# Another way of loading the first pair of contraction tiles, and row-block roots taken where they are used, in a 2048 x 2048 x 2048 matmul with RMS norm

## The chip, the cores and the metric

The kernel runs on one core of a Trainium2 chip. The metric is the device time of one execution in microseconds (us). The kernel before takes 224.4 us, the median of three runs from 224.26 to 224.63. The profiled execution is one of that kind. Engines are named as the profile names them: PE (TensorE matmul), PEld (its weight load), DVE (VectorE), ACT (ScalarE), POOL (GpSimd), SP (SyncE, which here only issues transfers).

## The reference

```python
m, k, n = 2048, 2048, 2048
x = np.matmul(a, b)
rms = np.sqrt(np.mean(x ** 2, axis=-1, keepdims=True) + eps)
return (gamma * x / rms).astype(np.float32)
```

All inputs and the output are float32 in DRAM. Each row of the product is divided by its own root mean square and multiplied by gamma.

## The kernel before

The 2048 rows are 16 row blocks of 128 rows; the contraction is 16 tiles of 128, taken in eight pairs `kp`. B has a left half (`j=0`) and a right half (`j=1`) of 1024 columns each, or four chunks of 512.

**The head (blocks 0 to 3, plain matmuls).** For each pair `kp`, `load_head` (L105) issues on POOL's software queue a load of A (four blocks by 256 columns, cast to bf16) and a load of B (256 rows by 1024 columns, cast to bf16). POOL issues in program order, and the trace shows that a ninth load waits until the first of the eight before it has landed. The pair 0 is loaded otherwise: A as float32 by SP's hardware queue (L92), B as float32 in two transfers by ACT's hardware queue (L94). `transpose_first` (L143) transposes the float32 A on PE into two PSUM banks, and DVE and ACT cast B (L151, L153) and DVE moves the transposed A to SBUF (L154). Eleven matmuls on zeros (L138) run ahead of it. Then `stream` (L364) runs for every `kp` seven output chunks for each of the two tiles, 14 matmuls; for the next pair's A, eight transposes (`transpose_head`, L160) stand between. The eighth chunk has no accumulating bank: `stream_in_parts` (L378) multiplies its two tiles into the bank `tbank`, which the transposes use too (there is one such bank), and ACT or DVE adds it to x in SBUF. When the left half is done, the same happens for the right half; in it DVE also forms sums of quarters of B (`b_sums`, `b_sums_in_place`, `b_sum_7`), and blocks 4 and 5 are normalised, cast (`prepare`) and transposed on PE by `transpose_half` (L174), again through the one `tbank`.

**The groups (blocks 4 to 15, two blocks each, seven products instead of eight).** `group_half(g, j)` (L483) forms a 2 x 2 block product from seven products of eight matmuls each, in the order 2, 5, 1, 4, 3, 7, 6. Their left operands are sums of quarters of A (`a_sums`, L238, on DVE), their right ones sums of quarters of B. Product 4 accumulates into the bank of product 2, and so must wait until ACT has copied product 2 out (the copy `c`, L498); product 3 likewise waits for DVE's L502, which reads the bank of product 5. Between the products stand hooks 0 to 7, at which `hooks_of` (L535) puts other work: `row_norm` (ACT, squares of a block's rows, then a root), `row_factor` (DVE, four small instructions that wait for it), `apply` (ACT scales and casts a block, L231, then SP issues a transfer that transposes it, L186) and `finish(mb)` (the end of a block: DVE multiplies both halves by 1/rms and gamma, L340, and SP stores them). A group's loads are issued when the group before has written a certain chunk (`load_after`, L529). The last group has its own order (`last_group`).

**The roots.** The sum of a block's squares and its root are `take_rms` (L313): a reduction on DVE, then a square root on ACT. `finish` then needs only a reciprocal on DVE. In groups 3 to 6, `take_rms` of the blocks that will be finished in this group stands at hook 1 of the left half, before the next `row_norm`; elsewhere `finish` calls it itself. The engines take their instructions strictly in the order in which the program issues them, so this order decides who waits for whom.

Of the kernel before, what the change touches and what calls it, by code (L numbers as in the profile page):

```python
# [8 lines left out]
FP32 = mybir.dt.float32  # L9
# [8 lines left out]
def kernel(  # L18
# [13 lines left out]
    nc = tc.nc  # L32
    P = 128
# [30 lines left out]
    sums = [t_left, t_right]  # L64

    a0f = early[:, 0:2048].bitcast(FP32).rearrange("p (r k) -> p r k", r=HB)
    b0f = [early[:, 2048 + t * 2048:2048 + (t + 1) * 2048].bitcast(FP32) for t in range(2)]
    NAH = 6
    ah_slot = [early[:, 6144 + s * 1024:6144 + (s + 1) * 1024].rearrange("p (r k) -> p r k", r=HB)
               for s in range(NAH)]  # L70
# [20 lines left out]

    nc.sync.dma_start(out=a0f, in_=a[0:HB * P, 0:W2].rearrange("(r p) k -> p r k", p=P))  # L92
    for t in range(2):
        nc.scalar.dma_start(out=b0f[t], in_=b[t * P:(t + 1) * P, 0:HALF])  # L94

    def ah(kp):
        return ah_slot[(kp - 1) % NAH]
# [7 lines left out]
    def load_head(kp):  # L105
        nc.gpsimd.dma_start(  # L106
            out=ah(kp),
            in_=a[0:HB * P, kp * W2:(kp + 1) * W2].rearrange("(r p) k -> p r k", p=P))
        load_b(0, kp)
# [10 lines left out]

        nc.gpsimd.tensor_copy(out=pace, in_=src)

    load_head(1)
    identity_f = consts.tile([P, P], FP32, name="identity_f")
    make_identity(nc, identity_f)
    for kp in range(2, 4):
        load_head(kp)
    warm = sq_pool.tile([P, 2 * CH], BF16, name="sq")
    nc.vector.memset(warm, 0.0)
# [4 lines left out]


    warm_bank = ps_a.tile([P, CH], FP32, name="acc")
    for _ in range(11):
        nc.tensor.matmul(warm_bank, warm[:, 0:P], warm[:, 0:CH], start=True, stop=True)  # L138

    gamma_sb = consts.tile([P, N], FP32, name="gamma_sb")  # L140
# [2 lines left out]
    def transpose_first():  # L143
        bank = [ps_t.tile([P, CH], FP32, name="tbank"), ps_a.tile([P, CH], FP32, name="acc")]
        view = [b.rearrange("p (r m) -> p r m", r=HB) for b in bank]
        for t in range(2):
            for r in range(HB):
                nc.tensor.matmul(view[t][:, r, :], a0f[:, r, t * P:(t + 1) * P], identity_f,
                                 is_transpose=True, start=(r == 0), stop=(r == HB - 1))
        for t in range(2):  # L150
            cast_first = [lambda: nc.vector.tensor_copy(out=raw[0][0][:, t, :CH],  # L151
                                                        in_=b0f[t][:, :CH]),
                          lambda: nc.scalar.copy(out=raw[0][0][:, t, CH:], in_=b0f[t][:, CH:])]  # L153
            move = [lambda h=h: nc.vector.tensor_copy(  # L154
                out=head_at[:, t, 2 * h:2 * h + 2, :], in_=view[t][:, 2 * h:2 * h + 2, :])
                for h in range(2)]
            for work in (cast_first + move if t == 0 else move + cast_first):
                work()

    def transpose_head(kp):  # L160
        bank = ps_t.tile([P, CH], FP32, name="tbank")
# [146 lines left out]
    def x_chunk(mb, c):  # L308
        return x_tile(mb, c // 2)[:, (c % 2) * CH:(c % 2 + 1) * CH]

    rms_of = {}

    def take_rms(mb):  # L313

        tot = stat_pool.tile([P, 1], FP32, name="tot")
        nc.vector.reduce_sum(out=tot, in_=msq.pop(mb), axis=mybir.AxisListType.X)
        rms_of[mb] = stat_pool.tile([P, 1], FP32, name="rms")
        nc.scalar.activation(out=rms_of[mb], in_=tot, func=ACTF.Sqrt)

    def inverse(rms):  # L320
        r = stat_pool.tile([P, 1], FP32, name="r")
        nc.vector.reciprocal(out=r, in_=rms)  # L322
        return r

    def inverse_rms(last, partial):

        rms = stat_pool.tile([P, 1], FP32, name="rms")
        nc.scalar.activation(out=rms, in_=last, func=ACTF.Sqrt, bias=partial, scale=1.0)
        return inverse(rms)

    def rows(mb, lo, hi):
        return out[mb * P:(mb + 1) * P, lo:hi]

    def finish(mb, order=(0, 1)):
        if mb not in rms_of:
            take_rms(mb)
        r = inverse(rms_of.pop(mb))
        for h in order:
            x = x_half.pop((mb, h))
            nc.vector.scalar_tensor_tensor(  # L340
                out=x, in0=x, scalar=r, in1=gamma_sb[:, h * HALF:(h + 1) * HALF],
                op0=ALU.mult, op1=ALU.mult)
            nc.sync.dma_start(out=rows(mb, h * HALF, (h + 1) * HALF), in_=x)
# [17 lines left out]
            kind, which = later.pop(0)  # L361
            load_b(1, which) if kind == "b" else load_block(which)

    def stream(groups, kp, before=(), when=None):  # L364


        order = [(g, kt) for kt in (2 * kp, 2 * kp + 1) for g in groups]
        if kp == KP - 1 or (kp == 0 and not before):
            order.sort(key=lambda x: groups.index(x[0]))
        for n, (g, kt) in enumerate(order):  # L370
            if n == (when or len(groups)):
                for work in before:
                    work()
            if kt == 0:
                banks[g] = new_bank()
            head_matmul(banks[g], *g, kt)
# [24 lines left out]
    for kp in range(KP):  # L401
        if kp + 4 < KP:
            load_head(kp + 4)
        else:
            load_later(1)
        before = [lambda: transpose_head(kp + 1)] if kp + 1 < KP else []
        stream(groups1, kp, before, len(groups1) + 5 if kp == 0 else None)
        if kp == KP - 1:
            evict(groups1, (1, 3, 5))
        stream_in_parts(last1, kp)  # L410
        if kp > 0:
            b_sums(0, kp - 1)
    load_later(2)
    b_sums(0, KP - 1)
# [16 lines left out]
    for kp in range(KP):  # L431
        load_later(1)
        before = [lambda: transpose_half(HB, 0)] if kp == 6 else []
        if kp == 7:
            before = [lambda: transpose_half(HB, 1)]
        stream(groups2, kp, before)
        square(squares[kp][0], x_chunk(*squares[kp]))
        if kp == 4:
            prepare(HB)
        if kp == 6:  # L440

            prepare(HB + 1)
        elif kp == KP - 1:
            b_sums_in_place(0, kp - 1)
        else:
            b_sums_2(kp)
    nc.gpsimd.dma_start(out=gamma_sb, in_=gamma.partition_broadcast(P))
    load_block(HB + 2)
    load_block(HB + 3)
# [10 lines left out]
    for kt in range(KT):  # L460
        if kt in (0, 6):
            transpose_half(HB + 1, kt // 6)
            if kt == 0:
                b_sums(1, KP - 2)
                b_sum_7(1, KP - 2)
        head_matmul(bank, r3, 3, kt)
    evict(groups2[-1:], ())
    row_norm(HB + 2)
# [66 lines left out]
    def hooks_of(g, j):  # L535


        hooks = {n: [] for n in range(8)}
        nxt = 2 * g + 2

        def hook(n, work, *args):
            hooks[n].append(lambda: work(*args))

        def apply(mb):
            row_apply(mb)
            transpose_dma(mb)

        more = g + 1 < NG
        if j == 0:
            if g == G0:  # L550
                hook(0, row_factor, nxt)
                hook(1, row_norm, nxt + 1)
                hook(1, apply, nxt)
                hook(2, a_sums, g, (7, 6))
                hook(2, row_factor, nxt + 1)
                hook(2, finish, 1)
                hook(3, squares2, 2)
                hook(4, apply, nxt + 1)
# [178 lines left out]
```

## Time and profile before

| | |
|---|---|
| median of three runs | 224.4 us |
| the profiled execution: time / span of its instructions | 224.4 / 222.6 us |
| PE busy | 211.1 us (95%) |
| DVE busy | 161.8 us (73%) |
| ACT busy | 129.1 us (58%) |
| POOL busy | 24.5 us (11%) |
| moved by transfers | 47.13 MB, mean 212 GB/s |

The span begins with the first instruction and ends with the last; 1.8 us of the execution lie outside it. Times in the trace count from the span's start. A line of the timeline gives start, duration, engine, source line, operation, what it writes and reads, how many instructions, and in brackets how long the engine sat idle before it and what ended that.

### The profile page before, as it was taken

What the parts mean: (1) busy time and instruction counts of PE and PEld (TensorE: products, weight loads), DVE (VectorE), ACT (ScalarE), POOL (GpSimd) and SP (SyncE); (2) the same over time, 40 slices, a digit from 0 to 9 for tenths busy, and PEclk for the clock granted to TensorE, in tenths of its full rate; (3) what the DMA queues carried; (4) which work ended last, traced back from release to release, by engine and by line L of the source; (5) the groups of instructions that cost most, each with busy time, mean ns of one, the idle gap of its engine ahead of it and who ended that gap; (6) DMA issues with size and microseconds to landing.
All of it is one profiled execution on the core that took longest, in us unless ns stands there. A gap on an engine that the chain in (4) does not pass through costs nothing.

```text
span 222.6 us, 3026 instructions
## 1 busy us (share of the span) xinstructions
PE 211.1 (95%) x1043; PEld 98.6 (44%) x1043; DVE 161.8 (73%) x324; ACT 129.1 (58%) x272; POOL 24.5 (11%) x49
## 2 busy tenths in 40 slices
PE   7899999999999999999999999999999999999950
PEld 2445444444454444444444444444444444444430
DVE  2427557983999989978949298837994589587692
ACT  3110002807698895799646985699478954334570
POOL 7534232300000001000100002000200000000000
PEclk9999999999999999999999999999999999999997
DMA  6999999999973499818889259945994794044045
GB/s 184 223 202 209 203 208 211 212 303 259 327 280 159 188 272 292 310 72 226 276 228 400 58 174 222 366 151 143 246 368 168 97 282 189 0 188 193 0 190 188
DMA packets 36176, 47.13 MB, mean 212 GB/s; under 512 B 21952, under 2 KB 26048, under 8 KB 34496
## 3 DMA queue, kind: packets, MB, share of 16 engines
q0 software_dynamic: 9648, 23.33, 41.6%
q1 hardware_dynamic: 26080, 22.29, 33.0%
q10 hardware_dynamic: 432, 1.31, 2.0%
q8 instruction: 8, 0.13, 0.2%
q14 instruction: 8, 0.07, 0.1%
HBM read 34.60 MB, written 16.78 MB: 231 GB/s over the span
## 4 chain that ended last, share of the span: by engine, by line
PE 83%; DMA 8%; DVE 2%; POOL 2%; issue 1%; ACT 1%; DVEq 0%; ACTq 0%; POOLq 0%
PE acc L279 63%; PE acc L350 18%; DMA b<-in_b_dram 8%; POOL early L106 1%; DVE x L617 1%; POOL b L100 1%; DVE x L620 1%; PE tbank L179 1%; PE tbank L382 1%; PE tbank L165 1%; ACT sq L291 0%; DVEq L732 0%; ACT sq L682 0%; DVE x L690 0%; DVE r L322 0%
## 5 line engine op out<-in xcount | busy, mean ns | idle before, releaser
L279 PE MATMUL acc<-b,s 128*128 128x512 bf16 x376 | 83.3, 379 | 0.0
L279 PEld LDWEIGHTS <-s 128*128 128x128 f16 x472 | 46.2, 98 | 55.7 <-DVE s L244 0.2
L350 PE MATMUL acc<-b,head_at 128*128 128x512 bf16 x240 | 55.1, 379 | 0.6 <-DMA b<-in_b_dram 0.4
L291 ACT ACTIVATE sq<-x 128x512 bf16<-128x512 f32 x62 | 39.1, 631 | 10.9 <-DVE x L520 5.1
L340 DVE SCALAR_TENSOR_TENSOR x<-x,r,gamma_sb 128x1024 f32<-128x1024 f32 x28 | 34.7, 1282 | 0.8
L209 ACT ACTIVATE sq<-a 128x1024 bf16<-128x1024 f32 x24 | 25.4, 1057 | 16.8 <-DMA a<-in_a_dram 16.4
L350 PEld LDWEIGHTS <-head_at 128*128 128x128 bf16 x240 | 22.9, 98 | 26.7 <-issue 1.1
L393 ACT COPY x<-acc 128x512 f32<-128x512 f32 x11 | 5.9, 591 | 25.1 <-PE acc L350 25.1
L231 ACT ACTIVATE head_at<-a,s 128x2048 f16<-128x2048 f32 x10 | 19.9, 1990 | 0.0
L279 PEld LDWEIGHTS <-at_even 128*128 128x128 f16 x96 | 9.4, 98 | 11.5 <-issue 0.4
L279 PEld LDWEIGHTS <-head_at 128*128 128x128 f16 x96 | 9.4, 98 | 11.3
L100 POOL DMA_DIRECT2D b<-in_b_dram x15 | 10.6, 708 | 16.0 <-DMA b<-in_b_dram 13.2
L217 DVE TENSOR_SCALAR s<-norm 128x1 f32<-128x1 f32 x12 | 1.8, 150 | 14.3 <-ACT norm L212 14.2
L244 DVE TENSOR_TENSOR s<-at_even 128x1024 f16<-128x1024 f16 x15 | 9.7, 684 | 2.8 <-DMA at_even<-head_at 2.8
L291 ACT ACTIVATION_READ_ACCUMULATOR sq<-x 128x1 f32 x62 | 11.7, 188 | 0.0
L279 PE MATMUL acc<-t_left,s 128*128 128x512 bf16 x48 | 11.3, 379 | 0.0
L279 PE MATMUL acc<-early,s 128*128 128x512 bf16 x48 | 11.3, 379 | 0.0
L279 PE MATMUL acc<-early,at_even 128*128 128x512 bf16 x48 | 11.0, 379 | 0.0
L279 PE MATMUL acc<-t_left,at_even 128*128 128x512 bf16 x48 | 10.9, 379 | 0.0
L509 ACT COPY x<-acc 128x512 f32<-128x512 f32 x10 | 5.7, 575 | 8.9 <-PE acc L279 8.9
L279 PE MATMUL acc<-t_left,head_at 128*128 128x512 bf16 x48 | 10.8, 379 | 0.0
L279 PE MATMUL acc<-early,head_at 128*128 128x512 bf16 x48 | 10.8, 379 | 0.0
(86 smaller groups left out, 205.8 us busy)
## 6 DMA issues: line engine op xcount, KB each, us to landing
out_dram<-x SPq DMA_DIRECT2D x30, 512.0 KB, 3.1
a<-in_a_dram POOLq DMA_DIRECT2D x12, 1024.0 KB, 8.5
b<-in_b_dram POOLq DMA_DIRECT2D x15, 512.0 KB, 17.1
early<-in_a_dram POOLq DMA_DIRECT2D x7, 256.0 KB, 14.8
early<-in_b_dram ACTq DMA_DIRECT2D x2, 512.0 KB, 5.9
gamma_sb<-in_gamma_dram POOLq DMA_DIRECT2D x1, 1024.0 KB, 19.9
out_dram<-x SPq DMA_DIRECT2D x3, 256.0 KB, 3.5
early<-in_a_dram SPq DMA_DIRECT2D x1, 512.0 KB, 5.7
```

The costliest lines, as they stand in the source:

```text
L100: nc.gpsimd.dma_start(out=raw[j][kp], in_=b[kp * W2:(kp + 1) * W2, j * HALF:(j + 1) * HALF].rearrange("(t p) n -> p t n", p=P))
L106: nc.gpsimd.dma_start(out=ah(kp), in_=a[0:HB * P, kp * W2:(kp + 1) * W2].rearrange("(r p) k -> p r k", p=P))
L165: nc.tensor.matmul(view[:, t, r, :], ah(kp)[:, r, t * P:(t + 1) * P], identity, is_transpose=True, start=(t == 0 and r == 0), stop=(t == 1 ...
L209: nc.scalar.activation(out=junk, in_=a32[mb][:, h * HALF:(h + 1) * HALF], func=ACTF.Square, scale=2.0 ** -8, accum_out=n2[:, h:h + 1])
L231: nc.scalar.activation(out=a16[mb], in_=a32.pop(mb), func=ACTF.Copy, scale=factor.pop(mb))
L244: nc.vector.tensor_tensor(out=s_sum[s], in0=x, in1=y, op=op)
L279: nc.tensor.matmul(bank, lhsT[:, kp, :], rhs, start=(start and kp == 0), stop=(kp == KP - 1), skip_group_check=not start)
L291: nc.scalar.activation(out=sq[:, 0:CH], in_=src, func=ACTF.Square, scale=inv_sqrt_n, accum_out=msq[mb][:, c:c + 1])
L340: nc.vector.scalar_tensor_tensor(out=x, in0=x, scalar=r, in1=gamma_sb[:, h * HALF:(h + 1) * HALF], op0=ALU.mult, op1=ALU.mult)
L350: nc.tensor.matmul(bank, head_at[:, kt, r, :], head_rhs(c, kt), start=(kt == 0), stop=(kt == KT - 1))
L393: copy(out=x_chunk(*g), in_=banks[g])
L509: nc.scalar.copy(out=x21, in_=p2)
```

## The change

In the head, B of pair 0 is no longer loaded as float32 and cast by DVE and ACT: POOL's software queue casts it in two transfers, and these are POOL's first. The load of A and B of pair 1 moves behind the making of the identity matrix. The warm-up has 8 matmuls. The transposed A of the first tile is moved by DVE, that of the second by ACT. In pair 0, the eighth chunk is multiplied after the seven matmuls of the first tile, and the transposes of pair 1 come three matmuls later, where they stood five later and the eighth chunk last.

At the end of the right half, `b_sums(1, 6)` and `b_sum_7(1, 6)` come before the last evictions instead of behind the first transposes of block 5.

In groups 3 to 6, the reduction and the root of a block are taken inside `finish`, never ahead of it; `row_factor` of the group's second new block moves from hook 2 to hook 3, and in group 3 `finish(3)` stands first at hook 2.

```diff
-    b0f = [early[:, 2048 + t * 2048:2048 + (t + 1) * 2048].bitcast(FP32) for t in range(2)]
...
     for t in range(2):
-        nc.scalar.dma_start(out=b0f[t], in_=b[t * P:(t + 1) * P, 0:HALF])
+        nc.gpsimd.dma_start(out=raw[0][0][:, t, :], in_=b[t * P:(t + 1) * P, 0:HALF])
...
-    load_head(1)
     identity_f = consts.tile([P, P], FP32, name="identity_f")
     make_identity(nc, identity_f)
-    for kp in range(2, 4):
+    for kp in range(1, 4):
         load_head(kp)
...
-    for _ in range(11):
+    for _ in range(8):
...
         for t in range(2):
-            cast_first = [lambda: nc.vector.tensor_copy(out=raw[0][0][:, t, :CH],
-                                                        in_=b0f[t][:, :CH]),
-                          lambda: nc.scalar.copy(out=raw[0][0][:, t, CH:], in_=b0f[t][:, CH:])]
...
+            move = (nc.vector.tensor_copy, nc.scalar.copy)[t]
+            for h in range(2):
+                pair = slice(2 * h, 2 * h + 2)
+                move(out=head_at[:, t, pair, :], in_=view[t][:, pair, :])
...
-    def take_rms(mb):
...
+    def inverse_rms(last, partial=None):
+
+        rms = stat_pool.tile([P, 1], FP32, name="rms")
+        if partial is None:
+            tot = stat_pool.tile([P, 1], FP32, name="tot")
+            nc.vector.reduce_sum(out=tot, in_=msq.pop(last), axis=mybir.AxisListType.X)
+            nc.scalar.activation(out=rms, in_=tot, func=ACTF.Sqrt)
+        else:
+            nc.scalar.activation(out=rms, in_=last, func=ACTF.Sqrt, bias=partial, scale=1.0)
         r = stat_pool.tile([P, 1], FP32, name="r")
         nc.vector.reciprocal(out=r, in_=rms)
         return r
...
     def finish(mb, order=(0, 1)):
-        if mb not in rms_of:
-            take_rms(mb)
-        r = inverse(rms_of.pop(mb))
+        r = inverse_rms(mb)
...
-            if n == (when or len(groups)):
+            if n == len(groups) + late:
                 for work in before:
                     work()
+            if late and n == len(groups):
+                stream_in_parts(last1, kp)
...
-        stream(groups1, kp, before, len(groups1) + 5 if kp == 0 else None)
+        stream(groups1, kp, before, 3 if kp == 0 else 0)
         if kp == KP - 1:
             evict(groups1, (1, 3, 5))
-        stream_in_parts(last1, kp)
         if kp > 0:
+            stream_in_parts(last1, kp)
             b_sums(0, kp - 1)
...
-        elif kp == KP - 1:
-            b_sums_in_place(0, kp - 1)
         else:
-            b_sums_2(kp)
+            b_sums_2(min(kp, KP - 2))
...
             transpose_half(HB + 1, kt // 6)
-            if kt == 0:
-                b_sums(1, KP - 2)
-                b_sum_7(1, KP - 2)
...
-                done = [2 * g - 2, 2 * g - 1]
+                if g == G0 + 1:
+                    hook(2, finish, r3)
                 hook(0, row_factor, nxt)
                 hook(1, apply, nxt)
-                if g == G0 + 1:
-                    hook(2, finish, r3)
-                    done.insert(0, r3)
-                for mb in done:
-                    hook(1, take_rms, mb)
                 hook(1, row_norm, nxt + 1)
-                hook(2, row_factor, nxt + 1)
+                hook(3, row_factor, nxt + 1)
                 hook(4 if g == G0 + 1 else 3, finish, 2 * g - 2)
```

More of the change, by code (lines that the diff above doesn't have):

```diff
@@ L150, in transpose_first @@
         for t in range(2):
-            cast_first = [lambda: nc.vector.tensor_copy(out=raw[0][0][:, t, :CH],
-                                                        in_=b0f[t][:, :CH]),
-                          lambda: nc.scalar.copy(out=raw[0][0][:, t, CH:], in_=b0f[t][:, CH:])]
[L154 to L158, printed above, removed]
+            move = (nc.vector.tensor_copy, nc.scalar.copy)[t]
+            for h in range(2):
+                pair = slice(2 * h, 2 * h + 2)
+                move(out=head_at[:, t, pair, :], in_=view[t][:, pair, :])
     def transpose_head(kp):
@@ L309, in x_chunk @@
         return x_tile(mb, c // 2)[:, (c % 2) * CH:(c % 2 + 1) * CH]
-    rms_of = {}
-    def take_rms(mb):
[L315 to L320, printed above, removed]
+    def inverse_rms(last, partial=None):
[6 more added lines that the diff above has]
+            nc.scalar.activation(out=rms, in_=last, func=ACTF.Sqrt, bias=partial, scale=1.0)
         r = stat_pool.tile([P, 1], FP32, name="r")
@@ L323, in inverse @@
         return r
[L325 to L329, printed above, removed]
     def rows(mb, lo, hi):
@@ L362, in load_later, with stream @@
             load_b(1, which) if kind == "b" else load_block(which)
-    def stream(groups, kp, before=(), when=None):
+    def stream(groups, kp, before=(), late=0):
         order = [(g, kt) for kt in (2 * kp, 2 * kp + 1) for g in groups]
```

## The prediction

> **What bounds the kernel now.** I read the chain of work that ended last, then the transfers by queue in the head, then the timeline at the three places that the change touches. The chain in order of time:
>
> ```profile
> 7.18 17.47 DMA b<-in_b_dram
> 24.64 0.04 issue
> 24.69 1.67 PE acc L350 x7
> ...
> 69.41 140.08 PE acc L279 x648
> ```
>
> Until 24.64 the chain is loading; from 24.69 to 209.5 it is PE without a gap, at 1.73 us for a product of eight matmuls. So a microsecond counts in two forms: PE starts earlier or later on the loads, or PE gets a wait that it does not have now. The other engines have slack, and it must be read at each place.
>
> The queues in the first 6.6 us (packets, MB, share of 16 engines), and the head's timeline:
>
> ```profile
> q10 hardware_dynamic: 201, 0.76, 40.7%
> q1 hardware_dynamic: 528, 0.52, 23.7%
> q0 software_dynamic: 3, 0.00, 0.2%
> ```
>
> ```profile
> 1.25 0.88 POOL L106 DMA_DIRECT2D early<-in_a_dram  x1 [0.80 <-POOLq L718]
> ...
> 10.00 0.77 POOL L106 DMA_DIRECT2D early<-in_a_dram  x1 [2.08 <-DMA early<-in_a_dram]
> ...
> 12.38 1.67 PE L350 MATMUL acc<-b,head_at 128*128 128x512 bf16 x7
> ...
> 12.63 0.70 POOL L100 DMA_DIRECT2D b<-in_b_dram  x1 [1.86 <-DMA b<-in_b_dram]
> 13.85 0.77 POOL L106 DMA_DIRECT2D early<-in_a_dram  x1 [0.52 <-DMA early<-in_a_dram]
> ...
> 16.32 0.70 POOL L100 DMA_DIRECT2D b<-in_b_dram  x1 [1.71 <-DMA b<-in_b_dram]
> ```
>
> POOL issued its first load at 1.25, yet the software queue moved three packets before 6.6, while the hardware queues had the engines. POOL's waits show when loads land: A of pair 1 by 10.00, B by 12.63, the next by 13.85 and 16.32. So a pair takes 3.85 (10.00 to 13.85), an A about 1.35, a B 2.5. PE needs 3.9 for a pair (18.24 to 22.14) and trails the loads by a few tenths, with one 0.4 wait at 24.69. Loads and PE are in step, and whatever moves the loads moves PE.
>
> The end of the right half, on DVE and PE, then the left half of group 3 on ACT, DVE and PE:
>
> ```profile
> 64.44 0.68 DVE L269 TENSOR_TENSOR b<-b 128x1024 bf16<-128x1024 bf16 x1
> 65.55 0.69 DVE L183 COPY at_even<-tbank 128x1024 f16<-128x1024 f16 x1 [0.43 <-PE tbank L179]
> 66.16 1.09 DVE L254 TENSOR_TENSOR early<-b 128x512 bf16<-128x512 bf16 x3
> ...
> 66.65 0.61 PE L179 MATMUL tbank<-identity_h,x 128*128 128x128 f16 x8
> ```
>
> ```profile
> 100.46 0.16 DVE L322 RECIPROCAL r<-rms 128x1 f32<-128x1 f32 x1 [1.21 <-ACT rms L318]
> 102.87 0.29 ACT L212 ACTIVATE norm<-n 128x1 f32<-128x1 f32 x1
> 104.30 1.99 ACT L231 ACTIVATE head_at<-a,s 128x2048 f16<-128x2048 f32 x1
> 107.64 0.59 ACT L498 COPY x<-acc 128x512 f32<-128x512 f32 x1
> 110.90 3.62 PE L279 MATMUL acc<-early,head_at 128*128 128x512 bf16 x16
> 116.41 1.89 DVE L244 TENSOR_TENSOR s<-at_even 128x1024 f16<-128x1024 f16 x3 [2.79 <-DMA at_even<-head_at]
> ```
>
> The reader is to see small margins: `tbank` is free at 66.24 and PE wants it at 66.65; copy `c` of the right half is done at 108.2 and product 4 starts at 110.90, a slack of 2.7.
>
> **Part 1, the head.** Removed: two float32 loads on ACT's queue, four casts, three warm-up matmuls (0.43 each). These matmuls end at 5.38, with PE idle until 6.57, so their removal is worth nothing by itself. They start 0.43 apart until 4.0 and twice as fast from about 4.4, so eight end near 4.7 and still reach the faster pace. Added: two software loads, which together are one B, 2.5 of the queue, ahead of pair 1. POOL's issues are 0.7 to 0.9 each, and pair 1's are done by about 5, before the queue reaches them. The casts' cover goes nowhere: DVE and ACT idle there.
>
> What matters is T, when the software queue starts. B of pair 1 then lands at T + 2.5 + 3.85; now PE has it by 12.3. Earliest T: 1.25 plus the 1.8 that a later load on an idle queue took (issued 88.37, moving at 90.18) = 3.05; latest: as now, about 6.6. Now it began when SP's A (0.52 MB) had finished, at about 6.35. With A alone on hardware, starting at about 2 and at the 300 GB/s that q1 reached alone, A is through by 4.3, and the queue joins 0.3 to 1.0 later. I take T = 5.1, nearest to that row: B lands at 11.45, **0.85 earlier**. PE can follow: A's transposes from 4.9, first matmul near 6.9, pair 1 from about 11. Ends: 6.6 and a slow start, as the queue now takes until 8.4 to fill, cost up to 0.9; 3.05 gains at most 1.4, since A then shares packets with 4 KB rows of B as now, lands near 6.2, and PE itself reaches pair 1 at 11.4 (1.0), without the 0.4 wait later. The eighth chunk moved up is the same two matmuls, 0.43; its ACT copy (0.59) must free `tbank` before the transposes, which the three matmuls between (0.65) cover.
>
> Here the Trainium skill bears on T. "DMA: Bandwidth & Descriptors", Latency and other measured facts, gives a first byte after about 1 us on the software path and 0.6 on the hardware one. By that T would be 3.1 and the head part a gain of 1.4 instead of 0.85; the trace's first load, 5.4 from issue to data, does not agree.
>
> **Part 2, the end of the right half.** Three L254 (0.40 apart) and one L259 (0.34 until the next) move ahead of the L183 that frees `tbank`. DVE has no pause from 55.18 to 65.1, so L183 starts at 64.44 + 0.60 + 1.20 + 0.34 = 66.58 and ends at 67.27. PE's second transposes wait from 66.65 until 67.33: **0.68 later**. Bounds: 0.2 if DVE leads more, 0.9. The first sums of A then have room, since L183 and L244 follow at once: no second wait.
>
> **Part 3, the roots.** The instructions are the same; only waits change. At group 3, left half, `finish(3)` needs a root that now stands behind the second `row_norm` on ACT. That ends at 103.07, or 102.8 without the three roots ahead of it (0.28). Root 0.2, reciprocal at 103.05 instead of 100.46; the two L340 take 2.40, until 105.65; then L506 (0.60), `row_factor` (0.70), L511 (0.60) and block 4's reduction (0.15): 107.7. ACT has done its copy and square by 104.4 and now stands before block 4's root until 107.7, with `apply` of block 9, the copy of product 3 and the right half's `c` queued behind. So `apply` starts at 107.95 instead of 104.30; 1.89, 0.6 and 0.8 later `c` starts at 111.2 and ends at 111.8. PE wants product 4 at 110.90: **0.9 wait**.
>
> Next late is the transposed block 9. SP issues it behind block 4's stores, whose second L340 ends at 110.65 instead of 107.87; so 111.1 instead of 108.41. It then took 8.0 until L244 began (116.41). The same gives 119.1, the first sum 0.7 later at 119.8; PE starts group 4 at 117.8 (121.26 less two products), now 118.7. The wait is 1.1, or 0.3 with the 7.2 that the same step took in group 4; I take **0.7**. Then L525 is late by 3, so POOL's loads for group 5 are late by 2.5, and `row_norm` holds ACT before `c` in group 4: slack there was 0.9 (c done 122.08, product 4 at 122.98), and the like happens in its right half: **0.25** in both. From group 5 on one `finish` per half delays ACT by 1.0 against slacks of 1.9 and more: nothing. Sum 1.85, bounds 0 (all absorbed by slack I read too small) and 3.
>
> Moving `row_factor` to hook 3 lets L506 go first: its bank is needed only three products later, so nothing.
>
> **Sum** against the profiled execution (224.4, which is also the median): -0.85 + 0.68 + 1.85 = +1.7, so **226.1 us**. Tail and last group issue the same work in the same order: 0.
>
> **Rivals.**
> 1. The software queue needs its 5.4 us after the first issue whatever else runs. For it: that is all the trace shows of a first load. Against: the queue came alive just when A had ended. Head +0.9 instead of -0.85: 227.8. It decides from T = 5.95 on, where the head turns to a loss.
> 2. The queue starts promptly, T near 3. For it: 1.8 at 88.37. Against: 6.6. Head -1.4: 225.5. (By the skill's first byte this is the case to expect.)
> 3. Not slower: ACT's stand before block 4's root does not reach PE. For it: group 2 has two inline roots in its left half now, and `c` there keeps 1.7 of slack; PE has seven banks. Against: group 3 starts with ACT already late (its `c` ends at 97.06, 1.7 after product 2) and finishes one block more. Price: part 3 falls to 0, total -0.17: 224.2. It decides once less than 0.2 of the 1.85 is left. With rival 2 on top it is 223.7.
> 4. The head does not do what it says, as PE is held by pair 4's load as before: that is T = 5.95, head 0: 227.0, inside the range.
>
> **Chances.** Forecast 0.45, rival 1 0.2 (with rival 4), rival 2 0.12, rival 3 0.15, rivals 2 and 3 together 0.08. The measurement tells 0.2%, 0.45 us. Faster: 0.08 from the last and 0.06 from rival 3; same 0.1, 0.07 of it from rival 3 and the rest from the forecast's low end; slower the rest, 0.76. The range reaches from rival 3 to just past rival 1, 223.9 to 228.1; the forecast's own is 225.2 to 227.0.
>
> **What would show it.** Pair 1's matmuls at about 11.5 and software packets from about 5; a 0.7 gap on PE at the second transposes of block 5, released by DVE L183; ACT idle some 3 us before a root in group 3's left half, and PE waiting about 0.9 for ACT L498; PE waiting for L244 at the start of group 4. Wrong would be PE without waits after 70 us, or software packets only from 6.6.

## The result and the profile after

The changed kernel takes 227.84 us (median of four runs, 227.6 to 228.21) against 224.5 (224.26 to 224.63) for the kernel before in the same session: a ratio of 1.0151, 95% interval 1.0134 to 1.0169, or 3.3 us more. Forecast were 226.1, in a range from 223.9 to 228.1. The sign was right and the time lies inside the range, close to its upper end; the loss is twice the +1.7 that the sum gave. The profiled execution is the 227.6 one, with a span of 225.8 us (222.6 before), so it has to explain 3.2 us.

In the kernel after, the head's matmul is L335 (was L350), the groups' product L273 (L279), copy `c` L481 (L498), the sums of A L238 (L244), the move of `tbank` L177 (L183), the root L311 (L318), the reciprocal L315 (L322), `apply` L225 (L231), the transposing transfer L180 (L186), the load of B L99 and of A L105. The chain of work that ended last, its long pieces in order of time (start, duration, what):

```profile
8.86 16.01 DMA b<-in_b_dram
25.16 15.76 DMA b<-in_b_dram
41.20 21.04 DMA b<-in_b_dram
...
112.04 8.03 DMA at_even<-head_at
...
120.85 91.70 PE acc L273 x424
```

Before, PE carried the chain without a gap from 24.69 on. Now the loads of B carry it until 62.2, and a transposing transfer carries it at the start of group 4. PE's list of waits (total, times, longest, in us) says the same by name; first its one wait for a load before, then after:

```profile
PE acc L350 <- DMA b<-in_b_dram: 0.4, 1, 0.4
```

```profile
PE acc L335 <- DMA b<-in_b_dram: 3.5, 4, 1.4
...
PE acc L273 <- DVE s L238: 1.3, 1, 1.3
PE acc L273 <- ACT x L481: 0.5, 1, 0.5
...
PE tbank L173 <- DVE at_even L177: 0.2, 1, 0.2
```

**The head.** First the first 6.6 us of the queues (packets, MB, share of 16 engines), and the issue of B's first pair (KB each, median us from issue to landing):

```profile
q0 software_dynamic: 221, 0.41, 45.9%
q1 hardware_dynamic: 528, 0.52, 25.7%
...
b<-in_b_dram POOLq DMA_DIRECT2D x2, 256.0 KB, 6.2
```

The software queue, three packets before, has moved 221 packets by 6.6; its first two are at 3.3 us. But it moves them slowly. The stretches of the after kernel (busy time of PE, PEld, DVE, ACT, POOL; granted PE clock; share of the DMA engines; GB/s, in bytes as written):

```profile
4.00:6.00 2.00, 1.57 (x11) 1.18 (x10) 0.76 (x2) 0.39 (x2) 2.00 (x4) 1.00 0.98 130
6.00:8.00 2.00, 1.00 (x5) 0.48 (x5) 0.00 (x0) 0.25 (x1) 2.00 (x7) 1.00 1.02 129
8.00:10.00 2.00, 1.81 (x10) 0.65 (x8) 0.00 (x0) 0.59 (x1) 1.00 (x2) 1.00 1.30 207
```

The hardware queue's last packets are at 3.8, so from 4 to 8 us the software queue has the engines to itself and moves 130 GB/s; the same kind of load moves 207 from 8 us on. The timeline shows what PE makes of it:

```profile
1.24 1.21 POOL L93 DMA_DIRECT2D b<-in_b_dram  x2 [0.79 <-POOLq L697]
...
7.00 1.67 PE L335 MATMUL acc<-b,head_at 128*128 128x512 bf16 x7 [1.43 <-DMA b<-in_b_dram]
...
8.86 0.70 POOL L99 DMA_DIRECT2D b<-in_b_dram  x1 [0.56 <-DMA b<-in_b_dram]
...
10.18 0.77 POOL L105 DMA_DIRECT2D early<-in_a_dram  x1 [0.62 <-DMA early<-in_a_dram]
...
12.46 1.67 PE L335 MATMUL acc<-b,head_at 128*128 128x512 bf16 x7 [1.03 <-DMA b<-in_b_dram]
...
24.91 1.67 PE L335 MATMUL acc<-b,head_at 128*128 128x512 bf16 x7 [0.59 <-DMA b<-in_b_dram]
```

B of pair 0 lands by 7.0 and 8.86, A of pair 1 by 10.18, B of pair 1 by 12.46, where PE waits 1.03 for it. Pair 1 so starts where it did (12.38), although PE began its first matmul 0.7 earlier than before (7.00 against 7.71).

**The end of the right half.** PE and DVE:

```profile
62.28 1.67 PE L335 MATMUL acc<-b,head_at 128*128 128x512 bf16 x7 [0.46 <-DMA b<-in_b_dram]
...
65.04 0.68 DVE L263 TENSOR_TENSOR b<-b 128x1024 bf16<-128x1024 bf16 x1
65.64 1.09 DVE L248 TENSOR_TENSOR early<-b 128x512 bf16<-128x512 bf16 x3
...
67.11 0.68 DVE L177 COPY at_even<-tbank 128x1024 f16<-128x1024 f16 x1
67.84 0.61 PE L173 MATMUL tbank<-identity_h,x 128*128 128x128 f16 x8 [0.20 <-DVE at_even L177]
```

PE waits for the last pair of B, which it did not before, and then for `tbank`, which the sums hold up.

**Group 3, left half, and the start of group 4.**

```profile
103.99 0.16 DVE L315 RECIPROCAL r<-rms 128x1 f32<-128x1 f32 x1 [4.49 <-ACT rms L311]
...
108.67 0.20 ACT L311 ACTIVATE rms<-tot 128x1 f32<-128x1 f32 x1 [3.48 <-DVE tot L310]
...
111.90 0.57 ACT L481 COPY x<-acc 128x512 f32<-128x512 f32 x1
112.04 3.41 SPq L180 DMA_TRANSPOSE at_even<-head_at  x1
...
112.52 3.61 PE L273 MATMUL acc<-early,head_at 128*128 128x512 bf16 x16 [0.47 <-ACT x L481]
...
120.10 1.90 DVE L238 TENSOR_TENSOR s<-at_even 128x1024 f16<-128x1024 f16 x3 [2.26 <-DMA at_even<-head_at]
120.85 3.63 PE L273 MATMUL acc<-b,s 128*128 128x512 bf16 x16 [1.26 <-DVE s L238]
```

DVE stands 4.49 before block 3's reciprocal, ACT then stands 3.48 before block 4's root, `c` ends at 112.47, and PE waits 0.47 for it. The transposed block 9 comes at 120.10, and PE waits 1.26 for its sum.

The same places in both timelines, in us, and how far behind the forecast had PE there:

| PE starts | before | after | behind | forecast |
|---|---|---|---|---|
| pair 1 | 12.38 | 12.46 | +0.08 | -0.85 |
| pair 4 | 24.69 | 24.91 | +0.22 | -0.85 |
| last pair of the right half (before: seventh of the 13 matmuls from 60.14, 0.216 apart) | 61.43 | 62.28 | +0.85 | -0.85 |
| second transposes of block 5 | 66.65 | 67.84 | +1.19 | -0.17 |
| product 4 of group 3 | 110.90 | 112.52 | +1.62 | +0.73 |
| product 1 of group 4 | 121.26 | 124.31 | +3.05 | +1.43 |
| end of the span | 222.6 | 225.8 | +3.2 | +1.7 |

After group 4's start hardly anything is lost. At 62 us PE is 1.7 behind the forecast; what follows adds 2.35 (3.2 less 0.85) where the forecast had 2.53 (0.68 + 1.85).

### The profile page after: what moved, and what is told of

It reads as the page before. It is cut to its first block, busy times and chain, and to the rows that moved or that the text cites. A ratio compares the mean times of both kernels' runs of the same rounds, so it can differ in the third digit from the quotient of the medians.

```text
span 225.8 us, 3015 instructions
## 1 busy us (share of the span) xinstructions
PE 210.6 (93%) x1040; PEld 98.3 (44%) x1040; DVE 160.4 (71%) x320; ACT 128.9 (57%) x272; POOL 25.6 (11%) x51
## 4 chain that ended last, share of the span: by engine, by line
PE 41%; DMA 34%; issue 12%; DVE 6%; ACT 4%; POOL 1%; DVEq 0%; POOLq 0%; ACTq 0%
PE acc L273 41%; DMA b<-in_b_dram 26%; DMA a<-in_a_dram 4%; DMA at_even<-head_at 4%; DVE x L325 2%; DVE x L596 1%; ACT sq L203 1%; ACT head_at L225 1%; DVE x L599 1%; ACT sq L285 1%; ACT x L380 0%; POOL a L114 0%; DVE s L238 0%; DVE r L315 0%; DVE x L494 0%
## 5 line engine op out<-in xcount | busy, mean ns | idle before, releaser
L273 PE MATMUL acc<-b,s 128*128 128x512 bf16 x376 | 83.4, 379 | 1.3 <-DVE s L238 1.3
L273 PEld LDWEIGHTS <-s 128*128 128x128 f16 x472 | 46.1, 98 | 57.2 <-DVE s L238 1.8
L335 PE MATMUL acc<-b,head_at 128*128 128x512 bf16 x240 | 55.4, 379 | 3.5 <-DMA b<-in_b_dram 3.5
L335 PEld LDWEIGHTS <-head_at 128*128 128x128 bf16 x240 | 23.0, 98 | 29.6 <-issue 3.9
L380 ACT COPY x<-acc 128x512 f32<-128x512 f32 x11 | 5.9, 591 | 29.2 <-PE acc L335 29.2
L225 ACT ACTIVATE head_at<-a,s 128x2048 f16<-128x2048 f32 x10 | 19.9, 1990 | 0.0
L273 PEld LDWEIGHTS <-head_at 128*128 128x128 f16 x96 | 9.4, 98 | 12.0 <-issue 0.8
L273 PEld LDWEIGHTS <-at_even 128*128 128x128 f16 x96 | 9.4, 98 | 11.3
L99 POOL DMA_DIRECT2D b<-in_b_dram x15 | 10.6, 707 | 16.1 <-DMA b<-in_b_dram 13.8
L164 DVE COPY head_at<-tbank 128x1024 bf16<-128x1024 bf16 x7 | 4.8, 692 | 10.0 <-PE tbank L159 10.0
L273 PE MATMUL acc<-t_left,s 128*128 128x512 bf16 x48 | 11.3, 379 | 0.0
L273 PE MATMUL acc<-early,s 128*128 128x512 bf16 x48 | 11.3, 379 | 0.0
L238 DVE TENSOR_TENSOR s<-at_even 128x1024 f16<-128x1024 f16 x15 | 9.7, 684 | 2.3 <-DMA at_even<-head_at 2.3
L273 PE MATMUL acc<-early,head_at 128*128 128x512 bf16 x48 | 10.8, 379 | 0.5 <-ACT x L481 0.5
L120 POOL COPY pace<-x 128x1 f32<-128x1 f32 x4 | 0.7, 183 | 90.4 <-DVE x L508 90.4
L273 PE MATMUL acc<-early,at_even 128*128 128x512 bf16 x48 | 10.9, 379 | 0.0
L273 PE MATMUL acc<-t_left,head_at 128*128 128x512 bf16 x48 | 10.8, 379 | 0.0
L273 PE MATMUL acc<-t_left,at_even 128*128 128x512 bf16 x48 | 10.8, 379 | 0.0
```

The lines of the kernel that those rows point to most:

```text
L99: nc.gpsimd.dma_start(out=raw[j][kp], in_=b[kp * W2:(kp + 1) * W2, j * HALF:(j + 1) * HALF].rearrange("(t p) n -> p t n", p=P))
L164: nc.vector.tensor_copy(out=head_at[:, 2 * kp:2 * kp + 2, :, :], in_=view)
L225: nc.scalar.activation(out=a16[mb], in_=a32.pop(mb), func=ACTF.Copy, scale=factor.pop(mb))
L238: nc.vector.tensor_tensor(out=s_sum[s], in0=x, in1=y, op=op)
L273: nc.tensor.matmul(bank, lhsT[:, kp, :], rhs, start=(start and kp == 0), stop=(kp == KP - 1), skip_group_check=not start)
L335: nc.tensor.matmul(bank, head_at[:, kt, r, :], head_rhs(c, kt), start=(kt == 0), stop=(kt == KT - 1))
```

## The experiments

Each run is compared with runs of the kernel before on the same chip; chips differ between some of the runs.

### Each part alone

**head_only: part 1 alone on the kernel before.**

```diff
-    b0f = [early[:, 2048 + t * 2048:2048 + (t + 1) * 2048].bitcast(FP32) for t in range(2)]
...
-        nc.scalar.dma_start(out=b0f[t], in_=b[t * P:(t + 1) * P, 0:HALF])
+        nc.gpsimd.dma_start(out=raw[0][0][:, t, :], in_=b[t * P:(t + 1) * P, 0:HALF])
...
-    for _ in range(11):
+    for _ in range(8):
...
-        stream(groups1, kp, before, len(groups1) + 5 if kp == 0 else None)
+        stream(groups1, kp, before, 3 if kp == 0 else 0)
```

> The kernel before with part 1 alone. By the prediction, 0.85 us faster. By the reading of the trace after, the first B rows move at half the steady rate, pair 1 starts where it did, and B of the right half's last pair lands late: 0.2 to 0.9 us slower, with a wait of PE on a load of B near 62 us.

Measured: 225.89 us, ratio 1.0063 (1.0046 to 1.0081), that is +1.45. Its profiled execution (226.54) in the timeline, and one stretch of it with the columns as above:

```profile
9.16 3.09 PE L344 MATMUL acc<-b,head_at 128*128 128x512 bf16 x7 [2.79 <-DMA b<-in_b_dram]
```

```profile
10.00:12.00 2.00, 2.00 (x6) 0.66 (x5) 0.00 (x0) 0.00 (x0) 0.87 (x2) 0.50 1.16 201
```

B of pair 0 is later still than in the kernel after, PE idles 2.79 before its first matmul, and then runs on half the clock (0.50): seven matmuls take 3.09 where they took 1.67. So part 1 is a loss by itself, greater than both expectations, and it begins with B's late landing; how much of it the half clock adds is read under head_warm. The expected wait near 62 us is not in this profile: PE is already 2.0 late there.

**sums_only: part 2 alone.**

```diff
-        elif kp == KP - 1:
-            b_sums_in_place(0, kp - 1)
         else:
-            b_sums_2(kp)
+            b_sums_2(min(kp, KP - 2))
...
-            if kt == 0:
-                b_sums(1, KP - 2)
-                b_sum_7(1, KP - 2)
```

> The kernel before with part 2 alone. By the prediction 0.7 us slower: PE waits at the second transposes of block 5 for the DVE copy that frees tbank, from 66.65 to about 67.33. The rival reads the trace after, where that wait was 0.2 to 0.4: then at most 0.4 us slower.

Measured: 224.9, ratio 1.0019 (1.001 to 1.0028), +0.46, which is nearer to the rival's 0.4 than to the 0.7. PE's waits have the one that was forecast:

```profile
PE tbank L179 <- DVE at_even L183: 0.4, 1, 0.4
```

**roots_only: part 3 alone.**

```diff
-                done = [2 * g - 2, 2 * g - 1]
-                hook(0, row_factor, nxt)
-                hook(1, apply, nxt)
                 if g == G0 + 1:
                     hook(2, finish, r3)
-                    done.insert(0, r3)
-                for mb in done:
-                    hook(1, take_rms, mb)
+                hook(0, row_factor, nxt)
+                hook(1, apply, nxt)
                 hook(1, row_norm, nxt + 1)
-                hook(2, row_factor, nxt + 1)
+                hook(3, row_factor, nxt + 1)
```

> The kernel before with part 3 alone. By the prediction 1.85 us slower. By the trace after 2.0 to 2.2: 0.6 before product 4 of group 3's right half, 1.4 before the first product of group 4, nothing later. The rival that the engines' slack absorbs it: within 0.3 of before.

Measured: 226.81, ratio 1.0102 (1.0079 to 1.0125), +2.37; the interval, from +1.8 to +2.8, holds the 1.85 as well as the 2.0 to 2.2. Its timeline:

```profile
103.33 0.16 DVE L322 RECIPROCAL r<-rms 128x1 f32<-128x1 f32 x1 [4.42 <-ACT rms L318]
...
108.00 0.20 ACT L318 ACTIVATE rms<-tot 128x1 f32<-128x1 f32 x1 [3.48 <-DVE tot L316]
...
111.24 0.57 ACT L498 COPY x<-acc 128x512 f32<-128x512 f32 x1
111.37 3.45 SPq L186 DMA_TRANSPOSE at_even<-head_at  x1
...
111.86 3.61 PE L279 MATMUL acc<-early,head_at 128*128 128x512 bf16 x16 [0.53 <-ACT x L498]
```

`c` starts at 111.24 (forecast 111.2), the transposes are issued at 111.37 (forecast 111.1), the reciprocal is at 103.33 (forecast 103.05). PE's waits are 0.5 for `c` and 1.2 for L244 at group 4.

**head_and_sums: parts 1 and 2 together**, the two diffs above on the kernel before.

> The change with the roots taken early as before. If the parts add, it is the change less what the roots cost: 0.9 to 1.3 us slower than before. If PE's late load of B hides the second transposes' wait, it is slower than the part 1 kernel by less than 0.4; if not, by 0.7.

Measured: 225.99, ratio 1.0076 (1.0051 to 1.0102), +1.55. By the medians part 2, worth 0.46 alone, adds some 0.1 to part 1, but the intervals of the two kernels lie over each other almost wholly, so this is not shown. The parts, 1.45 + 0.46 + 2.37 = 4.3 when each is alone, come to more than the 3.3 of the whole; with the widths of these intervals that difference is at the edge of what can be told.

### Which of the roots costs the time

**root3_early: part 3, with the root of block 3 alone taken early again** (the other blocks' roots stay inside `finish`).

```diff
                 hook(0, row_factor, nxt)
                 hook(1, apply, nxt)
+                if g == G0 + 1:
+                    hook(1, take_rms, r3)
                 hook(1, row_norm, nxt + 1)
                 hook(3, row_factor, nxt + 1)
```

> The part 3 kernel with one root taken early again, block 3's in group 3. By the prediction's chain everything hangs on that root standing behind the second row_norm: its multiplies then start at 100.5 again, the right half's copy c is done near 109 and the transposed block 9 is there by 117: within 0.4 us of before, instead of 2.4 slower. The rival: block 4's root alone holds ACT for long enough, and one or both waits of PE stay, 1.2 to 2.4 us slower.

Measured: 224.3 against 224.37, ratio 0.9992 (0.9982 to 1.0002): part 3's whole cost is gone. In its timeline the late steps come earlier again:

```profile
100.61 0.16 DVE L322 RECIPROCAL r<-rms 128x1 f32<-128x1 f32 x1 [1.83 <-ACT rms L318]
...
105.29 0.20 ACT L318 ACTIVATE rms<-tot 128x1 f32<-128x1 f32 x1 [0.94 <-DVE tot L316]
...
108.52 0.57 ACT L498 COPY x<-acc 128x512 f32<-128x512 f32 x1
108.66 3.44 SPq L186 DMA_TRANSPOSE at_even<-head_at  x1
```

Moving one reduction and one root of 0.2 us ahead of the second `row_norm` brings block 4's root 2.7 and `c` 2.7 earlier. `c` still starts 0.9 later than the 107.64 of the kernel before, as block 4's root still holds ACT for 0.94, but PE's slack there covers it. The same instructions in the same number, and 2.4 us less. This is shown for block 3's root; the other eight roots of groups 3 to 6, left where the change has them, and `row_factor` at hook 3 cost nothing that this measurement tells.

### Why B of pair 0 comes late

The loads of part 1 were the open point: the queue starts early and moves slowly. Each of the next runs changes one suspect. In the profiles of the new head without the small load of head_touch, and with B of pair 0 in two pieces, the first piece lands between 6.96 us (the kernel after) and 9.29 (head_warm) and the second between 8.57 and 10.54, so a single landing tells little by itself.

**head_hold: part 1, and POOL issues nothing more until B of pair 0 has landed.**

```diff
+    wait_for(raw[0][0][:, 1, 0:1])
     for kp in range(1, 4):
         load_head(kp)
```

> The part 1 kernel, but POOL issues nothing more until both pieces of B of pair 0 have landed. If POOL's back-to-back issuing is what slows the first pieces (75 to 160 GB/s between 4 and 8 us, against 200 to 210 later), they move at about 200 GB/s and have landed by about 7. If the first rows of B are slow by themselves, they land at 8.5 to 9 as before. Either way pair 1 is late by some us and the time is worse than the part 1 kernel's.

Measured: 231.36 us (a single run). The total says little, since every later load is issued late; the reading is POOL's waiting copy, and two stretches with the columns as above:

```profile
8.63 0.18 POOL L120 CAST pace<-b 128x1 f32<-128x1 bf16 x1 [5.62 <-DMA b<-in_b_dram]
```

```profile
4.00:6.00 2.00, 2.00 (x9) 1.53 (x8) 0.06 (x1) 0.00 (x0) 0.00 (x0) 1.00 0.89 125
...
12.00:14.00 2.00, 1.48 (x12) 0.85 (x13) 0.69 (x1) 0.00 (x0) 2.00 (x7) 1.00 0.98 138
```

B's second piece lands at 8.57 with nothing issued behind it, as in the kernel after (8.57), but 1.8 earlier than in head_only (10.37), from which this run differs by the one line. From 4 to 6 us the queue moves 125 with POOL idle, so POOL's issuing beside the transfer is not all of the slowness. It is not cleared either: from 5 to 6 and from 6 to 7 the queue moves 143 and 152 here, 88 and 71 in head_only, 121 and 116 in the kernel after. And the slow rate comes back when POOL issues the held loads in a row, from 8.75 to 15.53: 138 from 12 to 14, 100 from 14 to 16, and 204 only from 17 on. So the first 8 us as such are not the cause.

**head_one_load: part 1, B of pair 0 in one load of 256 rows.**

```diff
-    for t in range(2):
-        nc.gpsimd.dma_start(out=raw[0][0][:, t, :], in_=b[t * P:(t + 1) * P, 0:HALF])
+    nc.gpsimd.dma_start(out=raw[0][0], in_=b[0:W2, 0:HALF].rearrange("(t p) n -> p t n", p=P))
```

> The part 1 kernel with B of pair 0 in one software load of 256 rows instead of two of 128. If the small piece is what is slow, it moves at about 200 GB/s from 4 and lands near 6.7. If the time or the rows are, it lands near 8.5 to 9, and PE's first matmul on data starts then.

Measured: 228.92 (a single run). PE's first matmul of the head starts at 10.32, 3.56 after it was ready, and the queue moves 106 and 124 GB/s in the stretches from 4 to 6 and from 6 to 8. The cut into two pieces is not the cause; it helps, as PE can begin on the first.

**head_warm: part 1 with 20 warm-up matmuls**, so that PE is busy until 7.36.

```diff
-    for _ in range(8):
+    for _ in range(20):
```

> The part 1 kernel with 20 warm-up matmuls instead of 8, so that PE is never idle for as long as 2.8 us before B of pair 0 lands. If the half clock after that wait is what part 1 costs, the clock stays full, the runs draw together and the kernel is 0.1 to 0.6 us slower than before, instead of 1.45. If the late loads alone cost it, it stays at 1.2 to 1.7.

Measured: 226.86, ratio 1.0102 (1.0072 to 1.0132), +2.5 (on another chip than head_only's +1.45), outside both expectations. Three lines of its profiled execution (227.85, a span of 226.0), and then the second transposes of block 5 in head_only's, where the kernel before has them at 66.65:

```profile
9.33 1.67 PE L344 MATMUL acc<-b,head_at 128*128 128x512 bf16 x7 [1.09 <-DMA b<-in_b_dram]
...
68.06 0.61 PE L173 MATMUL tbank<-identity_h,x 128*128 128x128 f16 x8
...
145.25 3.63 PE L273 MATMUL acc<-b,s 128*128 128x512 bf16 x16 [1.26 <-DVE s L238]
```

```profile
68.69 0.61 PE L173 MATMUL tbank<-identity_h,x 128*128 128x128 f16 x8
```

The clock is full (seven matmuls in 1.67) and the first one is as late as in head_only. The total hides what the head does: at the second transposes PE is 1.4 behind the kernel before, and in head_only 2.0. In head_only PE reaches pair 1 at 15.01, when its B has been there since 14.2; in head_warm at 14.40, as soon as it lands. So in these two profiles the late loads cost 1.4 of head_only's 2.0 and the half clock the other 0.6. What makes head_warm's total worse comes far behind the head: PE waits 0.3 at 126.56 and 1.26 at 145.25, at the start of group 5, for the sums of A, which wait for a transposed block. The profiles of head_one_load and head_and_sums have that wait too (1.1 and 0.8), those of head_only and after_root3 do not, though PE is late there as well; why is open.

**head_from_a: part 1, the first two software loads read rows of A instead of B.** The product then uses wrong numbers for the first pair, and only the times are of use.

```diff
-        nc.gpsimd.dma_start(out=raw[0][0][:, t, :], in_=b[t * P:(t + 1) * P, 0:HALF])
+        nc.gpsimd.dma_start(out=raw[0][0][:, t, :], in_=a[t * P:(t + 1) * P, 0:HALF])
```

> The part 1 kernel with the two first software loads reading the same rows and columns of A instead of B (so the product uses wrong numbers for B's first pair; shapes, sizes and queues are the same). If what is slow is the first reading of B in an execution, these loads move at about 200 GB/s and PE's first matmul on data starts by 7. If any 4 KB rows are slow in the first 8 us, the loads take as long as B's did, until 8 to 9.

Measured: 225.09 (a single run). The first matmul is at 7.63 after a wait of 1.95, and the stretches from 4 to 8 have 133 and 109 GB/s. The pieces land at 7.58 and 9.22, inside the range of B's. Rows of A, of which SP's load reads the first 256 columns, are about as slow as rows of B that nothing has read, so the matrix is not the cause as far as one run tells.

**head_touch: part 1, and ACT's hardware queue first fetches 16 numbers of each of the first 256 rows of B.**

```diff
+    touch = consts.tile([P, 2, 16], FP32, name="touch")
+    nc.scalar.dma_start(out=touch, in_=b[0:W2, 0:16].rearrange("(t p) n -> p t n", p=P))
     nc.sync.dma_start(out=a0f, in_=a[0:HB * P, 0:W2].rearrange("(r p) k -> p r k", p=P))
```

> The part 1 kernel with one small load more, first on ACT's hardware queue: 16 numbers of each of B's first 256 rows, used by nothing. If B's first rows are slow because nothing has read them before, the loads behind it run at about 200 GB/s and the kernel is up to 1 us faster than the part 1 kernel; if not, nothing changes, or the small load delays A by some tenths.

Measured: 224.86 against 224.36, ratio 1.001 (0.9997 to 1.0023), +0.5, where head_only had +1.45 on another chip; the intervals do not meet. The timeline:

```profile
6.86 1.67 PE L346 MATMUL acc<-b,head_at 128*128 128x512 bf16 x7 [0.27 <-DMA b<-in_b_dram]
...
12.59 1.67 PE L346 MATMUL acc<-b,head_at 128*128 128x512 bf16 x7 [0.97 <-DMA b<-in_b_dram]
```

B's first piece is there when PE is (a wait of 0.27). The stretch from 4 to 6 has 158 GB/s, that from 6 to 8 again 124, and pair 1 still waits 0.97. So with a small load ahead the first piece is there early and the rest is as slow. One profile does not show that the small load did it, since the kernel after had its first piece at 6.96 without one.

### The whole change with block 3's root early, without and with the small load

**after_root3: all three parts, block 3's root early**; the edit is that of root3_early, on top of the change.

> The whole change with one step taken back: the reduction and root of block 3 stand ahead of the second row_norm of group 3 again. If part 3 costs the same among the other parts as alone (2.4 us, all of it from that root), this lands 2.4 below the changed kernel, at +0.9 over the kernel before (ratio 1.004). If instead part 3 costs among the others what the difference of the whole change and of parts 1 and 2 together says (3.34 - 1.55 = 1.8), this lands at the +1.55 of parts 1 and 2 (1.007). Rival: PE reaches group 3 later than in the kernel before by the head's delay, and ACT and DVE do not, so that the root's place costs less here and more than +2 is left (1.009). In the profile no wait of PE for L481's copy or for L238 at group 4 should be left; the waits for B in the head and for L177 stay.

Measured: 225.99 against 224.58, ratio 1.005 (1.0032 to 1.0068); +1.4 by the medians. All of PE's waits beside that for the warm-up's data:

```profile
PE acc L344 <- DMA b<-in_b_dram: 2.4, 1, 2.4
...
PE tbank L173 <- DVE at_even L177: 0.2, 1, 0.2
```

The waits at groups 3 and 4 are gone, so with one root moved 1.9 of the change's 3.3 go (on another chip). This lies between the first two expectations, and the interval, from +0.7 to +1.5, holds the first and ends just below the second; the third, more than +2, falls. Its runs spread from 224.67 to 226.59, where the kernel before spreads over 0.6 beside it. The first matmul on B's first piece is at 8.61 here, at 9.16 in head_only and at 7.00 in the kernel after, so it is likely that the head lands B sooner or later from run to run; only one run of each has a profile.

**after_root3_touch: the same with the small load**, whose diff is that of head_touch.

> The same kernel as the one beside it, and ahead of A's load ACT's hardware queue fetches 16 numbers of each of the first 256 rows of B, as in the run with part 1 alone. Same chip, so this tells the small load's worth by itself. If the small load is what quickened B's first piece, this is about 0.9 us below the kernel beside it (that run stood at +0.5 over the kernel before, part 1 without it at +1.45), that is at 1.000 to 1.003 of the kernel before, with the first head matmul near 6.9 in place of about 7.0 to 9. Rival: the two earlier runs were on different chips, and the small load did nothing; then the two kernels of this pair agree within 0.3 us.

Measured: 225.24, ratio 1.0025 (1.0012 to 1.0039), +0.66 and 0.75 below the kernel beside it on the same chip, with the first head matmul at 6.88 in place of 8.61. The two intervals overlap by a little, so the rival (0.3 or less) is not excluded; with head_touch against head_only this is the second pair of that sign, and a gain from the small load is likely but not shown.

No version beat the kernel before. root3_early equals it, and each kernel with the new head is above it by its median; head_touch's interval reaches down to it.

## Why the prediction was right or wrong

**Part 1, -0.85 forecast, about +0.85 by 62 us in the kernel after and +1.45 alone: the step that failed is the 2.5 for B of pair 0 in "B of pair 1 then lands at T + 2.5 + 3.85".** T itself was too late by 1.8 (software packets from 3.3, forecast 5.1), which alone would have given a further gain. But B of pair 0 then took until 8.6, or 5.3 instead of 2.5, and the two terms that follow were right: A by 10.18, B by 12.46, together 3.8 where 3.85 was forecast. 3.3 + 5.3 + 3.8 = 12.4 instead of 11.45, which is pair 1 at +0.08. In head_only B of pair 0 took until 10.37. Why it is slow stays open. The 2.5 was read from POOL's waits after 10 us, when the queue runs at 200 and more; no row of the profile before shows a casting load of B in the first 8 us, and I carried the rate back without a bound of its own. The slow start was named only as a part of the end of +0.9, tied to T = 6.6. That the queue would wait until A had ended is not borne out: its first packets are at 3.3 and A's last at 3.8. It does start sooner with less on the hardware queues (6.4 before).

Of the rivals, the second (a prompt queue, T near 3) is right in its start and wrong in its time, 225.5; the first (227.8) has the measured time but not the cause, since the queue was not late. The Trainium skill ("DMA: Bandwidth & Descriptors", Latency and other measured facts) gives about 1 us to the first byte on the software path; here the first packets are 2.0 after the start of the issue at 1.24, so that the 3.1 worked out from it is nearer than the 5.1 that I took.

The loss after the head (+0.22 at pair 4, +0.85 at the last pair) was not forecast at all: PE had 0.4 of waits on the loads before and has 3.5 now. POOL's loads from 30 us on are issued 0.2 earlier than before (43.70 against 43.93 for gamma's), yet the last pair of B comes later to PE. From issue to landing that load takes 21.0, before 20.0. Why was not tried, and how much of this 0.6 belongs to the change stays open: roots_only, with the old head, has a gap of 0.28 at the same place, sums_only none.

**Part 2, +0.68 forecast, +0.46 alone and +0.34 in the kernel after.** The mechanism is as told: L248 and L253 ahead of L177, and PE waits at the second transposes for it. The term was too big because PE is ready later after the sums' start than I had it, and DVE is a little faster. In the kernel after, DVE needs 2.75 from L263 to the end of L177 (65.04 to 67.79; forecast 2.83), but PE is ready 2.45 after L263's start (66.19 plus six matmuls of 0.216, less 65.04), not 2.21 as before (66.65 less 64.44). PE comes late for the loads there. In sums_only, with the old head, DVE needs 2.74, PE is ready after 2.28, and its gap is 0.52 from start to start, less the 0.22 of a matmul.

**Part 3, +1.85 forecast, +2.37 alone and +1.86 in the kernel after (from +1.19 to +3.05).** The chain from the second `row_norm` by `finish(3)`, block 4's root and `apply` to `c` is right to 0.3 at every step of roots_only. Of its terms, 0.9 for `c` became 0.69 alone (PE's gap from start to start, less the 0.22 of a matmul) and 0.63 by the same measure in the kernel after (+0.43 in the table), since PE comes to product 4 later too (what runs ahead of it ends at 111.33 alone and at 112.05 in the kernel after, at 111.06 before); the 0.7 at group 4 became 1.37 and +1.43; the 0.25 for group 4's `c` became nothing. The 0.7 was a mean of 1.1 and 0.3. The transposes' step took 8.06 (112.04 to 120.10) and so repeated the 8.0 of the same block in the same place before, and not the 7.2 of another group: the nearest row was the right one, and its 1.1 is the better forecast. In the sum the errors of part 3 cancel in the kernel after, which is luck. Its rival, that ACT's stand would not reach PE, falls; root3_early shows that this stand is all that part 3 costs.

**The sum.** -0.85 + 0.68 + 1.85 = +1.7 became 0.85 + 0.34 + 1.86 = +3.05, and 0.15 at the end. Part 1 is off by 1.7, more than the whole difference, and part 2 by 0.3 the other way. The chances gave 0.76 to slower, rightly, but the head was counted as a gain in all but a fifth of the cases.

## What to carry to other kernels

A rate read from the middle of a kernel is not a rate for its first loads: where the profile before has no transfer of that kind at that place, bound it by the slowest row that lies near in time, and let the sign of the part stay open. When an instruction that costs 0.2 us is moved, look at what its engine does just ahead of the new place and at who stands behind it on the next engine; here a root behind one `row_norm` held DVE, then ACT, then PE, and then the next group's transposes, for 2.4 us in all. Of two rows for the same step take the one of the same place, and not their mean. Read an experiment at the place that it changes before its total: head_warm is worse than head_only in total and 0.6 better in the head.

## What the runs showed of the hardware

The casting loads of B's and A's rows run at 71 to 133 GB/s (as written) between 4 and 8 us in the kernels without the small load, and at 190 to 215 from 10 us on (all but head_hold), with the DMA engines' share at 0.6 to 1.1 against 1.15 to 1.3. The cut into pieces and the matrix read were changed one by one, and it stayed; with POOL's other issues held back (head_hold) it was 125 from 4 to 6, and 138 and 100 from 12 to 16, when POOL issued them in a row. With the small load the stretch from 4 to 6 has 158 (head_touch) and 130 (after_root3_touch) against 117 (head_only) and 94 (after_root3). What the queue lacks is open; that POOL issues loads in a row at that time is a suspect that these runs do not clear.

PE's clock can fall to half in the head after a wait of 1.95 us (head_from_a), 2.4 (after_root3), 2.79 (head_only) or 3.56 (head_one_load), and then stays there for about 3.4 us by the granted clock of the stretches (in head_only 0.81, 0.50 and 0.83 from 8 to 14); after 3.08 in head_and_sums it stays for about twice as long (0.94, 0.50, 0.50, 0.50 and 0.85 from 6 to 16); waits of 1.09 in head_warm, 1.43 in the kernel after and even 2.24 in head_hold left it full. So the wait's length alone does not decide. The Trainium skill ("TensorE: Matmul & The Clock Gate", Part 1) gives a window of about 3.4 us that runs freely, which fits the length of the slow stretch; that a drop takes one idle window of that length, as it also says, does not agree with 1.95.
